# Last FFN of an encoder trunk: which PSUM sums its second projection keeps, and the order of its final norm

## The chip, the core and the metric

The kernel runs on one core of one Trainium2 chip. The metric is the device time of one execution in microseconds (us), the median of several runs. The profile comes from one further execution that the hardware profiler recorded. Its span runs from the first to the last instruction of the program on the core.

Names used below: TensorE (PE) multiplies matrices into PSUM, VectorE (DVE) and ScalarE (ACT) do elementwise work, GpSimd (POOL) and SyncE (SP) issue DMAs, and ACT can issue them too. Each engine works through its own queue in order.

## What is computed

The trunk has two layers. A layer is a half-step SwiGLU FFN, a gated pair of mixers, and another half-step FFN, each behind an RMSNorm and added to the residual x (512 tokens x 1024 columns, float32). Behind the last layer stands a final RMSNorm with a gain per column. The change is in the very last part of this:

```python
def rms_norm(x, g):
    xf = x.astype(jnp.float32)
    y = xf * lax.rsqrt(jnp.mean(xf * xf, axis=-1, keepdims=True) + RMS_EPS)
    return (y * g.astype(jnp.float32)).astype(x.dtype)

def swiglu(x, w_in, w_out):
    gu = x @ w_in
    g, u = jnp.split(gu, 2, axis=-1)
    return (jax.nn.silu(g) * u) @ w_out
...
        x = x + 0.5 * swiglu(rms_norm(x, ffn2_norm[l]), ffn2_w_in[l], ffn2_w_out[l])
    return rms_norm(x, final_norm)
```

## The kernel before

**Float32 by halves.** Every float32 operand is split into a high part and a low rest (`hi`, `lo`). A product of two of them is three matmuls: high by high (L508), low activations by high weights (L509), high activations by low weights (L511). For weights the split is made on the fly. Each granule of 128 x 1024 (some are 128 x 512) is loaded into a raw buffer (L148), ACT copies it to `whi` (L191), and DVE subtracts to get `wlo` (L194). Some granules are sums of two weight blocks: the second is added by an accumulating DMA from POOL (L150), or by DVE (L164). `whi` and `wlo` have three buffers each and raw nine, so a granule can be prepared at most about two granules ahead of PE. `Stream` walks a list of items in the order that `stage_items` (L199) wrote down. That list must match the order in which `product` (L513) asks for weights.

**The second projection of an FFN** multiplies 2816 features by 1024 columns with a Strassen-Winograd scheme: features, tokens and columns are each cut in two, and seven products take the place of eight. `x[j, i]` below is token half j (two blocks of 128 tokens) by column half i (512 columns). Each product runs over three chunks of features, c = 0, 1, 2, with two granules a chunk: 18 matmuls for c = 0 and 24 for c = 1 and 2. Each of them fills two PSUM banks, one for each block of 128 tokens.

The list `steps` (L758) sets the order: product 1 over its three chunks, product 2, then for each chunk 5, 6, 7, 3, and product 4 at the end. The operand of a step is combined by DVE (`comb`, L750), then split by ACT and DVE (L321, L322). `key` (L920) says which PSUM pair a product adds to: 6 goes on the sum of 1, and 4 on the sum of 7. Finished sums are added to x by `update` (L753, L756), one DVE instruction for each block:

| sum | goes to |
|---|---|
| 1 | x[0, 0], with a minus |
| 2 | x[0, 0] |
| 5 | x[1, 0], and x[1, 1] with a minus |
| 1 + 6 | x[1, 1]; x[1, 0] with a minus; x[0, 1] |
| 7 | x[1, 1] |
| 3 | x[1, 0] |
| 7 + 4 | x[0, 1] |

**The final norm.** `squares` (L371) has ACT sum the squares of one block and column half. Token half 1 (blocks 2 and 3) is complete before product 4 ends, token half 0 (blocks 0 and 1) only with it. The branch at L977 is written out by hand for DVE and ACT, and DVE comes to it behind the last `wlo`. For blocks 2 and 3, `inverses` (L445) makes the factor 1/rms in small steps. `gained` (L1022) multiplies half a row by the gain on DVE, `scaled` (L1029) multiplies a whole row of 1024 by 1/rms on ACT, and SP stores it (L1033). For blocks 0 and 1, `terms` (L424) prepares what is known of the first column half, and `inverse` (L431) finishes the factor: a square root on ACT, then four small DVE instructions (L438, L439, L441, L442). Block 0 ends with `gained` twice and `scaled`. Block 1 ends with `whole` (L1035) twice, a DVE instruction that applies gain and factor to half a row, and SP stores each half (L1040).

The last step, product 4 with c = 2, is done one token block after the other (`by_block`), so that block 0 is complete 12 matmuls before block 1.

**What orders the rest.** Outside of parts that are written out by hand, the order on ACT and DVE is the choice of a compile-time scheduler that goes by program order and readiness. At run time that order is fixed.

Of the kernel before, what the change touches and what calls it, by code (L numbers as in the profile page):

```python
# [14 lines left out]
AF = mybir.ActivationFunctionType  # L15
ALU = mybir.AluOpType
# [3 lines left out]
D = 1024  # L20
# [19 lines left out]
PLACE = {f: (h, c, i) for h in range(2) for c in range(3) for i, f in enumerate(CHUNK[h][c])}  # L40

# [49 lines left out]
def encoder_kernel(  # L91
# [107 lines left out]
    def stage_items():  # L199
# [39 lines left out]
        def ffn(s):  # L239
            first = not items  # L240
            if first:
                for g in range(4):
                    add(Raw((s, "cl", g)), parts=2 if g < 2 else 1, pieces=2 if g == 0 else 1)
            for j in range(NB):
                order = (1, 2, 5, 6, 7, 3, 4) if first and j == 0 else (1, 5, 6, 2, 7, 3, 4)
                strassen(s, lambda q: q, j, (1024,) * (2 if first or j else 3), order)
            for order in ((1,), (2,), (5, 6, 7, 3), (4,)):
                for c in range(3):
                    strassen(s, lambda q: "o" + q, c, out_sizes(c), order)
# [108 lines left out]
    class Norm:  # L358
# [65 lines left out]
        def terms(self, tb):  # L424

            e, f = small("e", 1), small("ef", 1)
            V.tensor_scalar(e, self.ssq[:, tb : tb + 1], 1.0 / D, EPS, ALU.mult, ALU.add)
            V.tensor_scalar(f, e, -0.5, None, ALU.mult)
            return e, f
# [185 lines left out]
    def stage_ffn(norm, nxt, late):  # L615
# [142 lines left out]
        steps = []  # L758
        for c in range(3):
            steps.append((1, c, lambda c=c: part(0, 0, c)))  # L760
        for c in range(3):
            steps.append((2, c, lambda c=c: part(1, 0, c)))
        for c in range(3):
            steps.append((5, c, lambda c=c: comb(part(0, 0, c), part(0, 0, c), part(0, 1, c), ALU.subtract)))
            steps.append((6, c, lambda c=c: comb(part(0, 0, c), part(0, 0, c), part(1, 1, c), ALU.add)))
            steps.append((7, c, lambda c=c: comb(part(0, 1, c), part(0, 1, c), part(1, 1, c), ALU.subtract)))
            steps.append((3, c, lambda c=c: part(1, 1, c)))
        for c in range(3):
            steps.append((4, c, lambda c=c: comb(part(1, 0, c), part(1, 0, c), part(0, 0, c), ALU.subtract)))
        made = {}  # L770

        def make(i):
            if i < len(steps) and i not in made:
                m, c, f = steps[i]
                made[i] = hl(f(), c, f"c{m}")
# [142 lines left out]
        for i, (m, c, _) in enumerate(steps):  # L918
# [3 lines left out]
            key = {6: 1, 4: 7}.get(m, m)  # L922
            if key not in ps:
                ps[key] = pair(f"o{key}")
            if m == 4 and c == 0 and nxt.mix:
# [4 lines left out]
                ps[key], made.pop(i), list(range(len(CHUNK[0][c]))), c == 0 and m in (1, 2, 3, 5, 7), c == 2,  # L930
                m in (4, 6), by_block=late and i == len(steps) - 1,
# [19 lines left out]
            if m == 4 and c == 1:  # L951
                update(ps[1], 1, 0, 1)
            if m == 4 and c == 0 and late:
                gf[0] = slot(F32, "gf", (D,))
                nc.sync.dma_start(out=gf[0], in_=bass.AP(tensor=gfin.tensor, offset=gfin.offset, ap=[[0, P], [1, D]]))
            if c < 2:
                continue
            if m == 1:
                update(ps[1], 0, 0, -1)
            elif m == 2:  # L960
                update(ps[2], 0, 0, 1)
                nxt.squares(0, 0)
            elif m == 5:
                update(ps[5], 0, 1, 1)
                update(ps[5], 1, 1, -1)
            elif m == 6:
                update(ps[1], 1, 1, 1)
            elif m == 7:
                update(ps[7], 1, 1, 1)
                nxt.squares(1, 1)  # L970
                update(ps[1], 0, 1, -1)
            elif m == 3:
                update(ps[3], 0, 1, 1)
                nxt.squares(0, 1)
                if late:
                    make(i + 3)
# [52 lines left out]
    def scaled(norm, tb):  # L1029
# [3 lines left out]
        nc.sync.dma_start(out=to, in_=o_)  # L1033

# [953 lines left out]
```

## Time and profile before

| what | value |
|---|---|
| time, median of 3 runs | 1858.4 us (1857.83 to 1858.85) |
| time of the profiled execution | 1859.64 us |
| its span, first to last instruction | 1857.9 us |
| PE busy | 1842.2 us (99% of the span) |
| DVE busy | 1605.6 us (86%) |
| ACT busy | 1311.2 us (71%) |
| POOL busy | 171.3 us (9%) |
| granted TensorE clock | 0.999 |

The profiled execution took 1.7 us more than its span, and 1.2 us more than the median of the runs. In the timeline view a row reads: start, duration, engine, line, operation, out<-in, shapes, count, and in brackets the idle time before it with what ended it. Where a row stands for several instructions (x2, x4), start is that of the first and the duration is from there to the end of the last. In tile names, `c5h` and `c5l` are the split operand of product 5, `o` on PE is the PSUM pair, `o` on DVE or ACT an output row, and `x` the residual.

### The profile page before, as it was taken

How to read it: one execution, taken by the hardware profiler on the slowest of the kernel's cores; microseconds unless marked ns; L12 is line 12 of the kernel's file. 1: busy time of each engine (PE TensorE's matmuls, PEld its weight loads, DVE VectorE, ACT ScalarE, POOL GpSimd, SP SyncE). 2: the span in 40 equal slices, each digit the busy share in tenths (PEclk: the TensorE clock that was granted, in tenths of full speed). 3: DMA queues.
4: the chain of work that ended last, by engine and by line, in shares of the span. 5: the costliest groups of instructions: out<-in, count | busy, mean ns of one | idle time of the engine just before them, and what ended most of it. 6: DMA issues, size and time to landing. Idle time of an engine off the chain costs nothing.

```text
span 1857.9 us, 24616 instructions
## 1 busy us (share of the span) xinstructions
PE 1842.2 (99%) x8862; PEld 1530.1 (82%) x8862; DVE 1605.6 (86%) x1950; ACT 1311.2 (71%) x1780; POOL 171.3 (9%) x210
## 2 busy tenths in 40 slices
PE   9999999999999999999999999999999999999997
PEld 7888878888888888888888888888888888888886
DVE  7878899786889987889998888998869899887898
ACT  6777875668676767777666778766675776777865
POOL 0001011100111010001010100101001101010010
PEclk9999999999999999999999999999999999999999
DMA  9898799932896788879888887988249867888794
GB/s 301 222 240 219 188 255 277 216 118 86 248 230 183 180 224 223 216 199 263 253 200 217 225 216 198 268 278 212 69 150 237 227 174 178 234 210 215 211 280 145
DMA packets 198458, 394.21 MB, mean 212 GB/s; under 512 B 103808, under 2 KB 103936, under 8 KB 198336
## 3 DMA queue, kind: packets, MB, share of 16 engines
q1 hardware_dynamic: 169664, 294.30, 49.2%
q0 software_dynamic: 28528, 98.33, 29.7%
q8 instruction: 69, 1.13, 0.3%
q14 instruction: 53, 0.43, 0.1%
q10 hardware_dynamic: 144, 0.02, 0.0%
HBM read 365.85 MB, written 2.11 MB: 198 GB/s over the span
## 4 chain that ended last, share of the span: by engine, by line
PE 88%; DVE 6%; DMA 2%; issue 2%; ACT 1%; SPq 0%; DVEq 0%; ACTq 0%
PE A L508 10%; PE A L511 10%; PE A L509 10%; PE B L509 5%; PE B L508 5%; PE B L511 5%; PE o L511 5%; PE o L509 5%; PE o L508 4%; PE ps L315 4%; PE ps L316 3%; PE ps L317 3%; PE C L508 3%; PE C L509 3%; PE C L511 3%
## 5 line engine op out<-in xcount | busy, mean ns | idle before, releaser
L194 DVE TENSOR_TENSOR wlo<-raw,whi 128x1024 fp32r<-128x1024 f32 (+1 forms) x534 | 632.0, 1195 | 172.8 <-ACT whi L191 171.3
L191 ACT ACTIVATE whi<-raw 128x1024 fp32r<-128x1024 f32 (+1 forms) x534 | 546.0, 1033 | 253.5 <-DVE raw L164 56.9
L150 POOL DMA_DIRECT2D raw<-in_wst_dram x166 | 144.2, 887 | 1339.3 <-DMA raw<-in_wst_dram 596.8
L164 DVE TENSOR_TENSOR raw<-raw,raw 128x1024 f32<-128x1024 f32 (+1 forms) x150 | 179.2, 1195 | 2.0
L509 PE MATMUL A<-whi,xl 128*128 128x512 f32 x400 | 155.7, 389 | 0.0
L508 PE MATMUL A<-whi,xh 128*128 128x512 f32 x400 | 155.7, 389 | 0.0
L356 ACT ACTIVATE at<-zt 128x1024 uint16<-128x1024 uint16 (+2 forms) x96 | 111.0, 1168 | 20.9 <-DMA zt<-zs 20.9
L186 ACT ACTIVATE whi<-raw 128x1024 fp32r<-128x1024 f32 (+1 forms) x83 | 85.9, 1035 | 46.9 <-issue 12.5
L511 PE MATMUL A<-wlo,xh 128*128 128x512 f32 x400 | 115.0, 389 | 0.0
L187 DVE SCALAR_TENSOR_TENSOR wlo<-raw,whi 128x1024 fp32r<-128x1024 f32 (+1 forms) x83 | 98.4, 1195 | 11.3 <-ACT whi L186 11.0
L511 PEld LDWEIGHTS A<-wlo,xh 128*128 128x128 f32 x400 | 75.1, 188 | 15.6
L508 PEld LDWEIGHTS A<-whi,xh 128*128 128x128 f32 x400 | 75.1, 188 | 15.4
L509 PEld LDWEIGHTS A<-whi,xl 128*128 128x128 f32 x400 | 75.1, 188 | 15.4
L508 PE MATMUL C<-whi,xh 128*128 128x512 f32 x208 | 81.1, 390 | 0.5 <-ACT whi L191 0.5
L509 PE MATMUL C<-whi,xl 128*128 128x512 f32 x208 | 81.0, 389 | 0.0
L509 PE MATMUL B<-whi,xl 128*128 128x512 f32 x208 | 81.0, 389 | 0.0
L508 PE MATMUL B<-whi,xh 128*128 128x512 f32 x208 | 80.9, 389 | 0.0
L730 ACT ACTIVATE th<-sn,rh 128x512 f32<-128x512 f32 x80 | 55.1, 715 | 36.2 <-DVE sn L583 35.4
L346 ACT ACTIVATE zs<-th 128x1024 uint16<-128x1024 uint16 x80 | 79.5, 1042 | 0.9 <-DVE th L737 0.9
L578 ACT ACTIVATE sn<-A 128x512 f32<-128x512 f32 x104 | 59.0, 584 | 24.9 <-PE A L511 24.9
L511 PE MATMUL B<-wlo,xh 128*128 128x512 f32 x208 | 59.8, 389 | 0.0
L511 PE MATMUL C<-wlo,xh 128*128 128x512 f32 x208 | 59.8, 389 | 0.0
(438 smaller groups left out, 4681.5 us busy)
## 6 DMA issues: line engine op xcount, KB each, us to landing
raw<-in_wst_dram SPq DMA_DIRECT2D x470, 512.0 KB, 5.7
raw<-in_wst_dram POOLq DMA_DIRECT2D x174, 512.0 KB, 8.0
raw<-in_wst_dram SPq DMA_DIRECT2D x30, 256.0 KB, 3.8
bm<-in_bias_dram SPq DMA_DIRECT2D x16, 384.0 KB, 3.5
x<-in_xin_dram SPq DMA_DIRECT2D x4, 512.0 KB, 10.2
raw<-in_wst_dram POOLq DMA_DIRECT2D x8, 256.0 KB, 8.4
dft<-in_dft_dram POOLq DMA_DIRECT2D x8, 256.0 KB, 4.3
gb<-in_gbias_dram SPq DMA_DIRECT2D x4, 512.0 KB, 14.8
```

The source lines that it names most:

```text
L150: G.dma_start(out=self.t, in_=wst[GRAN_AT[self.plus]][:, 0 : self.n], accum_op=ALU.add)
L164: V.tensor_tensor(self.raw.t, self.raw.t, self.add.t, ALU.add)
L186: S.activation(hi, t, AF.Copy, scale=-1.0)
L187: self.last = V.scalar_tensor_tensor(lo, t, -1.0, hi.bitcast(F32), ALU.mult, ALU.subtract)
L191: S.activation(hi[:, cs], t[:, cs], AF.Copy)
L194: self.last = V.tensor_tensor(lo[:, cs], t[:, cs], hi[:, cs].bitcast(F32), ALU.subtract)
L315: PE.matmul(ps, lh, rh, start=start, stop=False, skip_group_check=again)
L346: S.activation(s[:, h], words[:, h], AF.Copy)
L356: S.activation(to[:, w], t[:, w], AF.Copy)
L508: PE.matmul(ps, lh, rh, start=start, stop=False, skip_group_check=again)
L509: PE.matmul(ps, ll, rh, start=False, stop=False, skip_group_check=again)
L511: PE.matmul(ps, lh, rl, start=False, stop=stop, skip_group_check=again)
```

## The change

Four things change, all of them in the last FFN only (`late`), apart from code that is moved without effect.

1. Products 7 and 4 add to the PSUM pair of 1 and 6 (`key`). The sum 1 + 6 is read once, for x[1, 0]. After 7 it is read for x[1, 1], after 4 for x[0, 1]. So `update` is called twice less (four DVE instructions), and there is no pair for 7. Before product 7 may write the pair, the update after 6 must have read it, and before product 4 the update after 7.
2. The order of the products, of the weights and of their loads becomes: 1; 2 for c = 0, 1; 5, 6, 3 for each chunk; 7 for all chunks; 2 for c = 2; then 4. The chunk of product 2 stands between 7 and 4.
3. The factor for blocks 2 and 3 (`inverses`) and the prepared terms for blocks 0 and 1 (`terms`, now for both at once) are made during product 4, c = 0 and c = 1, ahead of the part that is written out by hand. The gain vector is loaded during product 7.
4. In the part written by hand, blocks 2 and 3 are finished first. For blocks 0 and 1, column half 0 is multiplied by the gain ahead of time and then scaled by ACT, which stores it from its own queue (`half_scaled`); column half 1 is finished by DVE (`whole`) and stored by SP.

```diff
+def out_order(last):
+
+    three = range(3)
+    if not last:
+        mid = [(m, c) for c in three for m in (5, 6, 7, 3)]
+        return [(1, c) for c in three] + [(2, c) for c in three] + mid + [(4, c) for c in three]
+    mid = [(m, c) for c in three for m in (5, 6, 3)] + [(7, c) for c in three]
+    return [(1, c) for c in three] + [(2, 0), (2, 1)] + mid + [(2, 2)] + [(4, c) for c in three]
...
-            for order in ((1,), (2,), (5, 6, 7, 3), (4,)):
-                for c in range(3):
-                    strassen(s, lambda q: "o" + q, c, out_sizes(c), order)
+            for m, c in out_order(s == (L - 1, 2)):
+                if m in (1, 2, 4, 5) or m == 7 and s == (L - 1, 2):
+                    group = {5: (5, 6, 3) if s == (L - 1, 2) else (5, 6, 7, 3)}.get(m, (m,))
+                    strassen(s, lambda q: "o" + q, c, out_sizes(c), group)
...
-            key = {6: 1, 4: 7}.get(m, m)
+            key = {6: 1, 7: 1 if late else 7, 4: 1 if late else 7}.get(m, m)
...
-            if m == 4 and c == 1:
+            if m == 4 and c == 1 and not late:
                 update(ps[1], 1, 0, 1)
-            if m == 4 and c == 0 and late:
+            if late and m == 7 and c == 1:
                 gf[0] = slot(F32, "gf", (D,))
...
+            if late and m == 4 and c < 2:
+                if c == 0:
+                    ready = nxt.inverses(2)
+                    next(ready)
+                    next(ready)
+                else:
+                    for _ in ready:
+                        pass
+                    ends = nxt.terms()
...
+                if late:
+                    make(i + 3)
...
+            elif m == 6 and late:
+                update(ps[1], 0, 1, -1)
             elif m == 6:
                 update(ps[1], 1, 1, 1)
             elif m == 7:
-                update(ps[7], 1, 1, 1)
+                update(ps[key], 1, 1, 1)
                 nxt.squares(1, 1)
-                update(ps[1], 0, 1, -1)
+                if not late:
+                    update(ps[1], 0, 1, -1)
...
-                    ready = nxt.inverses(2)
-                    next(ready)
-                    gained(2, 0)
-                    next(ready)
-                    gained(2, 1)
-                    for _ in ready:
-                        pass
-                    scaled(nxt, 2)
-                    update(ps[7], 1, 0, 1, (0,))
+                    for tb in (2, 3):
+                        gained(tb, 0)
+                        gained(tb, 1)
+                        scaled(nxt, tb)
+                    root = [nxt.inverse(b, *ends[b]) for b in range(2)]
+                    update(ps[1], 1, 0, 1, (0,))
                     nxt.squares(1, 0, (0,))
-                    root = [nxt.inverse(b, *nxt.terms(b)) for b in range(2)]
                     next(root[0])
-                    gained(3, 0)
-                    gained(3, 1)
-                    scaled(nxt, 3)
-                    update(ps[7], 1, 0, 1, (1,))
+                    gained(0, 0)
+                    gained(1, 0)
+                    update(ps[1], 1, 0, 1, (1,))
                     nxt.squares(1, 0, (1,))
                     next(root[1])
                     next(root[0])
-                    gained(0, 0)
                     next(root[0])
-                    gained(0, 1)
-                    scaled(nxt, 0)
+                    half_scaled(nxt, 0, 0)
+                    whole(nxt, 0, 1)
                     next(root[1])
                     next(root[1])
-                    whole(nxt, 1, 0)
+                    half_scaled(nxt, 1, 0)
                     whole(nxt, 1, 1)
...
+    def half_scaled(norm, tb, i):
+
+        o_, _, _, to = half(tb, i)
+        S.activation(o_, o_, AF.Copy, scale=norm.inv[tb])
+        S.dma_start(out=to, in_=o_)
```

In the file after the change, the added lines shift the numbers of those below them.

More of the change, by code (lines that the diff above doesn't have):

```diff
@@ L422, in gain, with terms @@
             return gn[:, c : c + 1]
-        def terms(self, tb):
-            e, f = small("e", 1), small("ef", 1)
-            V.tensor_scalar(e, self.ssq[:, tb : tb + 1], 1.0 / D, EPS, ALU.mult, ALU.add)
+        def terms(self):
+            e, f = small("e", 2), small("ef", 2)
+            V.tensor_scalar(e, self.ssq[:, 0:2], 1.0 / D, EPS, ALU.mult, ALU.add)
             V.tensor_scalar(f, e, -0.5, None, ALU.mult)
-            return e, f
+            return [(e[:, b : b + 1], f[:, b : b + 1]) for b in range(2)]
         def inverse(self, tb, e, f):
@@ L756, in update @@
                 V.scalar_tensor_tensor(v, ps[b], 0.25 * sign, v, ALU.mult, ALU.add)
[L758 to L769, printed above, removed]
+        operand = {
+            1: lambda c: part(0, 0, c),
+            2: lambda c: part(1, 0, c),
+            3: lambda c: part(1, 1, c),
+            5: lambda c: comb(part(0, 0, c), part(0, 0, c), part(0, 1, c), ALU.subtract),
+            6: lambda c: comb(part(0, 0, c), part(0, 0, c), part(1, 1, c), ALU.add),
+            7: lambda c: comb(part(0, 1, c), part(0, 1, c), part(1, 1, c), ALU.subtract),
+            4: lambda c: comb(part(1, 0, c), part(1, 0, c), part(0, 0, c), ALU.subtract),
+        }
+        steps = out_order(late)
         made = {}
@@ L773, in make @@
             if i < len(steps) and i not in made:
-                m, c, f = steps[i]
-                made[i] = hl(f(), c, f"c{m}")
+                m, c = steps[i]
+                made[i] = hl(operand[m](c), c, f"c{m}")
         def two(settle):
@@ L917, in stage_ffn @@
         ps = {}
-        for i, (m, c, _) in enumerate(steps):
+        for i, (m, c) in enumerate(steps):
             make(i)
@@ L929, in stage_ffn @@
             product(
-                ps[key], made.pop(i), list(range(len(CHUNK[0][c]))), c == 0 and m in (1, 2, 3, 5, 7), c == 2,
-                m in (4, 6), by_block=late and i == len(steps) - 1,
+                ps[key], made.pop(i), list(range(len(CHUNK[0][c]))), c == 0 and m in (key, 2), c == 2,
+                m != key, by_block=late and i == len(steps) - 1,
             )
@@ L974, in stage_ffn @@
                 nxt.squares(0, 1)
-                if late:
-                    make(i + 3)
             elif late:
```

## The prediction

> **What bounds the kernel now.** I read the page's totals first, then busy time by stretch around the end, then the timelines of the last FFN engine by engine.
>
> ```profile
> span 1857.9 us, 24616 instructions
> PE 1842.2 (99%) x8862; PEld 1530.1 (82%) x8862; DVE 1605.6 (86%) x1950; ACT 1311.2 (71%) x1780; POOL 171.3 (9%) x210
> ```
>
> ```profile
> 1754.00:1845.00 91.00, 91.00 (x403) 75.28 (x402) 89.25 (x95) 57.79 (x69) 10.03 (x12) 1.00 0.79 224
> 1848.40:1857.90 9.50, 0.00 (x0) 0.00 (x0) 4.97 (x14) 3.50 (x6) 0.00 (x0) 0.73 0.56 221
> ```
>
> PE is the bound: busy 99%, and in the second projection (first row, columns: length, then PE, PEld, DVE, ACT, POOL) 91.00 of 91.00 us. The change removes no matmul. So it can win only behind PE's end, in the 9.5 us of the second row, and it can lose wherever it makes PE wait. DVE with 89.25 of 91.00 us is next to full, so it is the engine that could do that. I work out the tail first, then the middle.
>
> **The tail.** PE's last matmul, two DVE and two ACT chains, and the stores:
>
> ```profile
> 1847.69 0.61 PE L511 MATMUL o<-wlo,c4h 128*128 128x512 f32 x2
> ```
>
> ```profile
> 1842.17 1.23 DVE L194 TENSOR_TENSOR wlo<-raw,whi 128x1024 fp32r<-128x1024 f32 x1
> ...
> 1847.62 1.28 DVE L1027 TENSOR_TENSOR o<-x,gf 128x512 f32<-128x512 f32 x2
> 1848.82 0.68 DVE L756 SCALAR_TENSOR_TENSOR x<-o,x 128x512 f32<-128x512 f32 x1
> ...
> 1850.63 0.68 DVE L1027 TENSOR_TENSOR o<-x,gf 128x512 f32<-128x512 f32 x1
> 1851.23 0.21 DVE L438 TENSOR_SCALAR mh<-ssq,ef 128x1 f32<-128x1 f32 x1
> ...
> 1852.10 1.42 DVE L1039 SCALAR_TENSOR_TENSOR o<-x,inv,gf 128x512 f32<-128x512 f32 x2
> ```
>
> ```profile
> 1848.94 1.15 ACT L1032 ACTIVATE o<-o,r 128x1024 f32<-128x1024 f32 x1 [0.21 <-DVE o L1027]
> 1849.99 0.61 ACT L375 ACTIVATE junk<-x 128x512 bf16<-128x512 f32 x1
> ...
> 1850.73 0.29 ACT L436 ACTIVATE sq<-ssq,e 128x1 f32<-128x1 f32 x1
> ```
>
> ```profile
> 1853.55 0.61 SPq L1040 DMA_DIRECT2D out_dram<-o  x1
> ```
>
> ```profile
> out_dram<-o SPq DMA_DIRECT2D x3, 512.0 KB, 2.6
> out_dram<-o SPq DMA_DIRECT2D x2, 256.0 KB, 2.9
> ```
>
> PE is through at 1847.69 + 0.61 = 1848.30; call this E. Before, three things then run late. DVE is still multiplying block 3 by the gain and starts the update of block 1 at 1848.82 (0.52 late). It ends at 1849.50, but ACT is scaling block 3 until about 1849.99 (0.45 late). Square root at 1850.73, out at 1851.02; DVE takes it at 1851.23, behind one more gain (0.21 late). The four small instructions take 1851.23 to 1852.10, 0.87. Then two halves, and the last store is issued at 1853.55.
>
> After, by the same durations. Behind the last `wlo` DVE has four gains (0.60 each, by 1.28 for two), 2.4 us, then the update of block 0, which is ready 12 matmuls or 2.7 us ahead of E, and two gains, 1.2 us. The last `wlo` ends at 1843.40 before. Were it no earlier, this would end at 1843.40 + 2.4 + 0.6 + 1.2 = 1847.6, ahead of E. The update of block 1 thus starts at E: 1848.30 to 1848.98. ACT's two scalings of 1.15 and the squares of block 0 are over before that too. So squares at 1849.02, 0.74 on (1849.99 to 1850.73) the root at 1849.76, out at 1850.05. DVE in the meantime: block 0's four small ones from 1848.90 to 1849.77, block 0's half (1.42 for two: 0.67 to the next start, 0.75 for the last) to 1850.44, block 1's four, 0.87, to 1851.31, and its half, 0.75, to 1852.06. Store issued near 1852.1: **1.45 us earlier** (0.52 and 0.45 of lateness gone, block 1's factor 0.18 later behind the root than before, one half of 0.67 out of the chain).
>
> ACT's halves beside this: 512 columns cost between the 0.61 of squares and the 1.15 of 1024 columns; I take 0.61, same size. Block 0's runs 1850.08 to 1850.7, then ACT issues its store. A store issued by ACT isn't in this tail; the nearest is a load that ACT issues at the start:
>
> ```profile
> 0.74 0.39 ACTq L1826 DMA_DIRECT2D gn<-in_gains_dram  x1
> ```
>
> That is 0.39, SP's last store 0.61; either way ACT is free by 1851.3, when block 1's factor is out, and its half ends at 1851.95 with the issue at 1852.0. Beside DVE's half, so free. Landing: before, the last three stores, one row of block 0 and two halves of block 1, crowd together; after, only the last two halves do, with block 0's 1.5 us ahead of them. By the two rows a store lands 2.6 us after issue by itself and 2.9 in the crowd, so 0 to 0.3 is won; I take 0.3. The tail gives **1.75 us**, or 1.45 without this.
>
> On that last 0.3 the Trainium skill speaks against it. Its page "DMA: Bandwidth & Descriptors", section "Issuing engines are not separate DMA queues", says that DMAs from SP and ACT run on the same 16 DMA engines and interleave, so a second issuing engine saves only the time to issue. By that the two last halves land together as half a MB would, the 0.3 shrinks towards 0, and the forecast below would read 1857.5. The rows lean that way (halves 2.9, whole rows 2.6), but can't show it, since no two queues store at once before.
>
> **The middle: does PE still never wait?** What the order costs is DVE's work against PE's.
>
> ```profile
> 1789.61 0.39 PE L508 MATMUL o<-whi,c5h 128*128 128x512 f32 x1
> ...
> 1805.96 0.39 PE L508 MATMUL o<-whi,c3h 128*128 128x512 f32 x1
> ```
>
> ```profile
> 1817.63 1.22 DVE L194 TENSOR_TENSOR wlo<-raw,whi 128x1024 fp32r<-128x1024 f32 x1
> 1818.77 2.48 DVE L756 SCALAR_TENSOR_TENSOR x<-o,x 128x512 f32<-128x512 f32 x4
> 1821.16 1.22 DVE L194 TENSOR_TENSOR wlo<-raw,whi 128x1024 fp32r<-128x1024 f32 x1
> ```
>
> Products 5, 6 and 7 of one chunk lie between the two PE rows: 72 matmuls in 16.35 us, 0.227 each, 5.45 a product. On DVE an instruction of 1024 columns takes the place of 1.14 us (1817.63 to 1818.77), an update 0.60 (four from 1818.77 to 1821.16).
>
> A chunk in the order 5, 6, 3 needs 6 `wlo`, 4 sums of weights, 3 rests of operands and 2 combinations: 15 x 1.14 = 17.1 us against 16.35 of PE, 0.75 short. With product 7 in it, as before, it is 19 x 1.14 = 21.7 against 21.8, even. For c = 0, with 0.87 and 0.60 for its smaller sizes, 13.05 against 54 x 0.227 = 12.25, 0.8 short. Then four updates after 5 and two after 6: 3.6. In all 0.8 + 2 x 0.75 + 3.6 = 5.9 us short when product 7 starts, and PE now must wait there for those two updates. Product 7 gives it back (4 x 1.14 = 4.55 against 5.45). Some of this is done ahead:
>
> ```profile
> 1744.89 0.95 DVE L750 TENSOR_TENSOR at<-at,at 128x768 f32<-128x768 f32 x1
> 1745.76 1.22 DVE L750 TENSOR_TENSOR at<-at,at 128x1024 f32<-128x1024 f32 x1
> ...
> 1757.58 1.22 DVE L750 TENSOR_TENSOR at<-at,at 128x1024 f32<-128x1024 f32 x1
> ```
>
> These three must be product 5's, by what they may read so early: 0.87 + 2 x 1.14 = 3.15. So 2.75 us short. And the lead that DVE has to lose, from a `wlo`'s end to its first matmul:
>
> ```profile
> 1769.59 1.22 DVE L194 TENSOR_TENSOR wlo<-raw,whi 128x1024 fp32r<-128x1024 f32 x1
> ...
> 1797.17 1.24 DVE L194 TENSOR_TENSOR wlo<-raw,whi 128x1024 fp32r<-128x1024 f32 x1
> ```
>
> ```profile
> 1775.10 1.07 PE L511 MATMUL o<-wlo,c5h 128*128 128x512 f32 x4
> ...
> 1798.68 0.63 PE L511 MATMUL o<-wlo,c6h 128*128 128x512 f32 x2
> ```
>
> At product 5's first granule it is 1775.10 - 1770.81 = 4.3 us, at 6's last of c = 1 it is 1798.68 - 1798.41 = 0.27. So the lead shrinks by 4.0 before, where the count above says even: DVE also takes up combinations that aren't due. After, 5 comes a product earlier (5.45) and only 3.4 (two `wlo`, one rest) + 1.2 of DVE's work moves behind it: 0.85 less. The bounds are then 4.3 - 0.85 - 2.75 = 0.7 us left, no stall, and 4.0 less than that, a stall of 3.3. I take **0.6 us of stall**, one update's slot, since the nearest row (0.27) shows a lead near nothing with no stall. The four updates that go save 2.4 us of DVE; on the path that is worth nothing, since PE doesn't wait for them, beyond the lead it restores behind product 7. A wait of product 7 costs its full length, since every later matmul stands behind it on PE. Product 4's wait for the update after 7 has a chunk of product 2, 5.45 us, in between: two updates (1.2) fit, so nothing.
>
> What moves behind product 7: its updates 1.2, those of product 2 1.2, and `inverses` and `terms`, eight small DVE instructions of at most 0.21 (the L438 row), 1.7; 4.1 in all. Spare there on DVE: 5.45 - 3.4 in product 2's chunk, 0.6, 0.9 and 0.9 in product 4's, 4.45. So they are hidden; without that cover the last `wlo` comes later, of which the first 0.7 (1847.6 against E) is free. ACT, 57.79 us of 91, has room for the squares that move. Of loads none is added; the gain vector's half MB moves into product 7, on SP's queue, and is counted in (b).
>
> **Sum.** 1857.9 - 1.75 + 0.6 = 1856.75 for the span, -1.15. The profiled execution took 1859.64, 1.2 above the median of 1858.4; I take the difference to the median: **1857.2**.
>
> **Rivals.**
> (a) *DVE runs out of lead and product 7 waits for its update.* The place is the end of 6 and 3, c = 2, and the start of 7, c = 0; it decides once the lead at 6, c = 2 is under the 3.6 of updates. For it: 0.27 before. Against: DVE's total is smaller. Price 3.3, so -1.75 + 3.3 = +1.55, 1859.9, slower; where the updates' 3.6 come on top, +5.15, 1863.5.
> (b) *Transfers.* Rows of the DMA view from 1780 to 1820 (packets, MB, share of the time of 16 engines):
>
> ```profile
> q0 software_dynamic: 1107, 4.01, 51.6%
> q1 hardware_dynamic: 2277, 8.06, 51.3%
> ```
>
> A granule of 0.52 MB takes 0.516 x 40 x 0.52 / 4.01 = 2.7 us when accumulated and 1.3 when loaded plainly. Product 7 needs two of each, 8.0 us against 5.45; three of them in a row fall 2.0 (c = 0) + 2 x 2.6 = 7.2 behind, and 1.3 more with the gain vector. The chunks of 5, 6, 3 (13.4 against 16.35) gain 2.9 each ahead of it, as far as nine buffers allow. If only one chunk's 2.9 is kept, beside half of the 4.3 of lead, 7.2 + 1.3 - 2.9 - 2.15 = 3.45 us of stall: +1.7, 1860.1; with neither, 8.5: +6.75, 1865.1.
> (c) *The tail is hardly shortened.* If an ACT half costs the whole row's 1.15 and each issue 0.61 of ACT's time, block 0's half and store hold ACT from 1850.08 to 1851.84, block 1's half ends at 1853.0, and the last store is issued 0.55 earlier than before, not 1.45. With the stall that is +0.05, 1858.4: the change then does nothing.
> (d) No stall, and all of the tail: 1856.6.
>
> **Chances.** Forecast (with d) 0.60, (a) 0.24, (b) 0.08, (c) 0.08. The likeliest case's own range is 1856.1 to 1858.6 ((d) less half a microsecond, the runs' own spread, to a stall of 2). For 8 in 10 I reach to (b), (c) and the cheaper (a): 1855.8 to 1861.2. Bounds of 0.2% (3.7 us), about what a measurement of this kernel can tell from no change, are 1854.7 and 1862.1: faster 0.05 (only what I overlook), slower 0.15 (the dear end of (a), and the rest of (b)), same 0.80.
>
> **What would show it.** The update of block 1 starts within 0.1 of PE's end, the squares directly behind it, the last store is issued 3.8 us behind PE's end (5.25 before). PE idle in the second projection is under 1.5 us; if there is more, the row behind the gap names DVE (a) or a DMA under ACT's `whi` (b). A last store later than 4.5 behind E shows (c). The forecast is wrong if the gaps are many, or if the tail keeps one of its three delays.

## The result, and the profile after

| kernel | median of its runs, us | ratio to before | 95% interval |
|---|---|---|---|
| before, beside it | 1858.12 (6 runs) | | |
| changed | 1864.68 (6 runs, 1862.43 to 1868.31) | 1.0034 | 1.0024 to 1.0045 |

The changed kernel is slower by 0.3%, outside the forecast range. Its profiled execution took 1862.43 us, the fastest of its six, so the profile shows the smaller part of the loss: a span of 1860.7 beside 1857.9, 2.8 us more. From the page's totals of the changed kernel:

```profile
PE 1843.1 (99%) x8862; PEld 1529.1 (82%) x8862; DVE 1603.4 (86%) x1944; ACT 1311.7 (70%) x1781; POOL 171.3 (9%) x210
```

The totals say nothing: PE is at 99% in both. The stretch of the second projection does (length, then PE, PEld, DVE, ACT, POOL). Before, PE was busy in 91.00 of these 91 us:

```profile
1754.00:1845.00 91.00, 86.98 (x374) 69.17 (x374) 85.05 (x95) 57.07 (x69) 8.63 (x10) 1.00 0.78 228
```

PE lacks 4.02 us, and DVE is busy for 85.05 us where it was 89.25 before: it is no longer full either. The view of PE's waits in that stretch (who waits, for whom, us in total, times, longest) has no row at all for the kernel before, and these for the changed one:

```profile
PE o L519 <- ACT c7h L332: 1.1, 1, 1.1
PE o L519 <- ACT whi L201: 1.1, 1, 1.1
PE o L522 <- DVE wlo L204: 1.1, 1, 1.1
PE o L520 <- DVE c7l L333: 0.7, 1, 0.7
```

There are four waits, at three places: near 1761, near 1790, and at product 7's last chunk near 1825. The timeline of the changed kernel around them, and around its end:

```profile
1744.44 9.83 SPq L358 DMA_TRANSPOSE zt<-zs  x2
1745.12 0.86 POOL L160 DMA_DIRECT2D raw<-in_wst_dram  x1 [41.58 <-DVE at L761]
1747.55 0.86 POOL L160 DMA_DIRECT2D raw<-in_wst_dram  x1 [1.57 <-DVE wlo L197]
...
1756.64 1.37 ACT L367 ACTIVATE at<-zt 128x1024 uint16<-128x1024 uint16 x1 [3.64 <-DMA zt<-zs]
...
1758.51 0.69 DVE L204 TENSOR_TENSOR wlo<-raw,whi 128x512 fp32r<-128x512 f32 x1 [3.55 <-ACT whi L201]
...
1761.63 0.50 PE L519 MATMUL o<-whi,c2h 128*128 128x512 f32 x1 [1.07 <-ACT whi L201]
...
1790.51 0.73 PE L522 MATMUL o<-wlo,c6h 128*128 128x512 f32 x2 [1.05 <-DVE wlo L204]
...
1823.64 1.06 ACT L201 ACTIVATE whi<-raw 128x1024 fp32r<-128x1024 f32 x1 [2.30 <-DMA raw<-in_wst_dram]
...
1824.61 1.04 ACT L332 ACTIVATE c7h<-at 128x1024 fp32r<-128x1024 f32 x1
...
1825.70 0.73 PE L519 MATMUL o<-whi,c7h 128*128 128x512 f32 x2 [1.14 <-ACT c7h L332]
1827.15 0.50 PE L520 MATMUL o<-whi,c7l 128*128 128x512 f32 x1 [0.72 <-DVE c7l L333]
...
1852.22 0.61 PE L522 MATMUL o<-wlo,c4h 128*128 128x512 f32 x2
1852.87 0.69 DVE L767 SCALAR_TENSOR_TENSOR x<-o,x 128x512 f32<-128x512 f32 x1 [0.82 <-PE o L522]
...
1855.88 0.72 ACT L1053 ACTIVATE o<-o,inv 128x512 f32<-128x512 f32 x1 [0.63 <-DVE inv L453]
...
1856.63 0.37 ACTq L1054 DMA_DIRECT2D out_dram<-o  x1
```

**The end** went as forecast. PE is through at 1852.22 + 0.61 = 1852.83. The update of block 1 starts 0.04 behind it, the last store is issued 3.80 behind it (5.25 before), and the span ends 7.87 behind it (9.60 before): 1.73 us won. But PE itself ends 4.53 us later than before's 1848.30, and 4.53 - 1.73 is the 2.8 of the span.

**Near 1761** the reader is to follow the chain upward. PE waits for a `whi` of ACT. ACT had stood 3.64 us, with that `whi` queued behind it, at the copy `at<-zt`, which waits for a pair of transposing DMAs, the first of them issued by SP at 1744.44. DVE stood 3.55 us for the same ACT. Beside SP's transposes POOL issues two accumulating loads, at 1745.12 and 1747.55. In the changed order of weights these are product 5's first two granules. Before, the same loads came behind the transposes:

```profile
1745.42 3.33 SPq L347 DMA_TRANSPOSE zt<-zs  x1
1749.48 3.47 SPq L347 DMA_TRANSPOSE zt<-zs  x1
1753.68 0.86 POOL L150 DMA_DIRECT2D raw<-in_wst_dram  x1 [47.67 <-DVE c1l L322]
1755.08 1.38 ACT L356 ACTIVATE at<-zt 128x1024 uint16<-128x1024 uint16 x1 [0.58 <-DMA zt<-zs]
1756.53 0.86 POOL L150 DMA_DIRECT2D raw<-in_wst_dram  x1 [1.99 <-DVE wlo L194]
```

The view of the tile `zt` gives the transposes' time from issue to landing, for the changed kernel and then for the one before:

```profile
DMA to landing us min/median/max: 8.6/8.8/9.0
```

```profile
DMA to landing us min/median/max: 5.3/5.4/5.6
```

Beside the accumulating loads the transposes take 3.4 us longer.

**At 1825** ACT waits 2.30 for a raw granule of product 7, `c7h` stands behind that `whi` in ACT's queue, and PE waits for `c7h` and then for DVE's `c7l`. The DMA view of the changed kernel from 1805 to 1826 (packets, MB, share of 16 engines' time):

```profile
q1 hardware_dynamic: 1278, 4.39, 53.3%
q0 software_dynamic: 580, 2.10, 50.5%
```

The two kinds add up to all that 16 engines have. The four accumulating loads, 2.10 MB, take 0.505 x 21 = 10.6 us, 2.65 a granule.

Counted from one matmul's start to the next, less the usual 0.227, the gaps of the changed kernel are 1.5 us near 1761, 1.2 near 1790, 2.2 near 1825 and 0.35 elsewhere, 5.2 in all, where the kernel before has one of 0.70 at 1752. Behind each gap one more interval is 0.1 longer. From its first matmul to its last the projection takes 111.08 us (1741.36 to 1852.44), before 105.57 (1742.35 to 1847.91): 5.5 us more. PE ends only 4.53 later because this execution came to the projection 0.99 earlier, from parts that are the same in both kernels.

The wait near 1790 can't be read from one profile: DVE is late with a `wlo`, and it may have been late by its own count or by the 3.55 us that it lost at 1758. That is for the experiments.

### The profile page after: what moved, and what is told of

It reads as the page before. It is cut to its first block, busy times and chain, and to the rows that moved or that the text cites. A ratio compares the mean times of both kernels' runs of the same rounds, so it can differ in the third digit from the quotient of the medians.

```text
span 1860.7 us, 24610 instructions
## 1 busy us (share of the span) xinstructions
PE 1843.1 (99%) x8862; PEld 1529.1 (82%) x8862; DVE 1603.4 (86%) x1944; ACT 1311.7 (70%) x1781; POOL 171.3 (9%) x210
## 4 chain that ended last, share of the span: by engine, by line
PE 88%; DVE 4%; DMA 3%; issue 3%; ACT 1%; POOL 0%; SPq 0%; DVEq 0%; ACTq 0%; POOLq 0%
PE A L519 10%; PE A L522 10%; PE A L520 10%; PE o L522 5%; PE o L520 5%; PE o L519 5%; PE B L520 5%; PE B L519 5%; PE B L522 5%; PE ps L326 4%; PE ps L327 3%; PE ps L328 3%; PE C L520 2%; PE C L519 2%; PE C L522 2%
```

## The experiments

The theory after this reading: two bursts of accumulating loads cost the time, one by holding up the transposes, one by being late themselves, and the wait at 1790 is an echo of the first. The rival: DVE's work ahead of product 7 is too much, as rival (a) of the prediction has it, and the loads are only beside it. Each time is compared with runs of the kernel before on the same chip: 1860.03 (23 runs) for the two halves, for the kernel without product 7's second block and for product 2 at its old place; 1859.46 (27) for the changed kernel once more, for the kernels without product 5's second block and without both, and for 7 and 2 in turn; 1859.21 (29) for product 5 summed by DVE, one chunk of 2 ahead, and the end with one issuing engine.

### The two halves of the change, each alone

The first kernel has the old order of products, weights and sums, and the new last rows; the second has the new order and the old last rows. The core of the first, against the changed kernel (the second is its counterpart):

```diff
-    mid = [(m, c) for c in three for m in (5, 6, 3)] + [(7, c) for c in three]
-    return [(1, c) for c in three] + [(2, 0), (2, 1)] + mid + [(2, 2)] + [(4, c) for c in three]
+    mid = [(m, c) for c in three for m in (5, 6, 7, 3)]
+    return [(1, c) for c in three] + [(2, c) for c in three] + mid + [(4, c) for c in three]
...
-            key = {6: 1, 7: 1 if late else 7, 4: 1 if late else 7}.get(m, m)
+            key = {6: 1, 4: 7}.get(m, m)
```

> The kernel before with only the norm's part of the change: factor and terms made early, blocks 2 and 3 first, the last rows in halves by ACT and DVE. Products, sums and weights keep their old order. Theory (the loss of the changed kernel is all in the middle, the tail gains 1.7): PE ends where it does before, from PE's end to the end of the span 7.8 us in place of 9.6, and the time is 1.5 to 1.8 us below the kernel before. Rival (the tail needs the four updates gone): DVE is late at the last weights, PE waits up to 1 us, and the gain is under 0.8 us.

> The changed kernel with the old order of the norm's tail: products 7 and 4 on the sum of 1 and 6 and the new order of weights alone. Theory: PE ends 4 to 7 us later than before, as in the changed kernel, and the time is 5 to 8 us above the kernel before. Rival (the early norm steps and the moved gain vector in the middle make the gaps): PE ends within 1.5 us of before, time within 1.5 us.

The new end alone: 1859.14 (11 runs), ratio 0.9996, 0.9987 to 1.0004. Its span is 1856.1, PE waits for nothing from 1754 on, as before, and from the last matmul's start to the span's end are 8.39 us, 9.95 before: 1.56 won. The median is 0.9 us below before, not the 1.5 to 1.8 expected; the interval holds both that gain (0.08%) and no change.

The new order alone: 1872.25 (5 runs), ratio 1.0061, 1.0048 to 1.0074. That is 11 to 12 us above before, more than the 5 to 8 expected, and PE's last matmul starts 7.5 later than before (1855.45). So the loss is in the order, and neither the early norm steps nor the new end are needed for it. Its waits in the profile are those of the changed kernel, at the same places (near 1762, 1790 and 1825 to 1828). But one thing is added behind the last one. The busy times of the stretch behind it (length, PE, PEld, DVE, ACT, POOL, then the granted clock, the DMA share and GB/s):

```profile
1829.50:1833.00 3.50, 3.50 (x10) 2.67 (x10) 2.73 (x4) 1.21 (x2) 0.00 (x0) 0.51 0.29 112
```

PE waits for nothing here, yet its granted clock is 0.51, and its matmuls start 0.427 us apart where they otherwise start 0.227 apart. That adds about 3.5 x (1 - 0.227 / 0.427) = 1.6 us.

### The changed kernel once more

> The changed kernel unaltered, for a second profile and on the same chip as the next three. Theory (part of the loss is PE's granted clock: where its waits in product 7 add up to about 2.4 us, the clock is halved for some 3.5 us behind them, 1.4 us more): the waits stand at the same places, near 1760, 1789 and 1825, and a profile that is longer than the first has a stretch of clock near 0.5 behind the last of them; time 4 to 8 us above the kernel before. Rival (the longer runs come from transfers alone): the clock stays at 1.00 throughout, and the longer profile has longer waits.

1866.41 (5 runs), ratio 1.0042, 1.0029 to 1.0055. This profiled execution, 1865.98 us, has the same waits near 1761 and 1790, and at product 7 a longer one, again with the low clock behind it. The two waits at 7 from the view of PE's waits, and the stretch behind them:

```profile
PE o L519 <- ACT c7h L332: 3.0, 1, 3.0
...
PE o L520 <- DVE c7l L333: 0.7, 1, 0.7
```

```profile
1829.50:1833.00 3.50, 3.50 (x11) 2.69 (x10) 2.64 (x3) 1.74 (x2) 0.00 (x0) 0.53 0.19 73
```

Here the two waits at 7 are 1.9 longer than in the first profile (3.0 beside 1.1), and the clock adds about 1.6. Together that is 3.5 of the 3.9 us by which the projection is longer (115.03 beside 111.08); the spans differ by 3.5 (1864.2 and 1860.7). Executions of this kind would lift the median above the first profile, but how many of the runs are like it no profile shows.

### Each burst without its accumulating loads

Three kernels leave the second weight block out: of product 7's granules, of product 5's first two, and of both. The order and all other work stay.

```diff
 # product 7
-            for q, q2 in (("a", None), ("b", None), ("c", "a"), ("d", "c")):
+            for q, q2 in (("a", None), ("b", None), ("c", None if order == (7,) else "a"), ("d", "c")):
...
 # product 5, c = 0
-            for q, q2 in (("a", None), ("b", None), ("c", "a"), ("d", "c")):
+            for q, q2 in (("a", None), ("b", None), ("c", "a"), ("d", None if order == (5, 6, 3) and idx == 0 else "c")):
```

> The changed kernel, but product 7's weights are loaded without adding their second block, so that part of its sum is left out. Three products 7 in a row then need 2.7 us of transfers each, not 8. Theory (transfers): the gap of 2.3 us at product 7, c = 2, goes, and the spread of the times with it; time 2 to 5 us below the changed kernel. Rival (DVE's lead): ACT and DVE are late at product 7 in any case, the gap stays over 1.5 us, and the time falls by less than 1 us.

> The changed kernel, but the two granules of product 5, c = 0, are loaded without adding their second block, so that part of its sum is left out. Theory (these two accumulating loads hold up the transposes, ACT waits 3.6 us behind them, and DVE idles with it): ACT's wait for the transposed words near 1753 falls under 1 us, the PE gap near 1760 goes, and the gap of 1.2 us near 1790 goes too, since it comes from the lead that DVE lost there; PE ends 2 to 2.7 us earlier than in the changed kernel. Rival (DVE's own count of work in 5, 6, 3 makes the gap near 1790): that gap stays, and PE ends only 0.8 to 1.5 us earlier.

> Both loads left plain: product 5's, c = 0, and all of product 7's, whose second blocks are left out of the sums. Theory (two bursts of accumulating loads make all of the loss): PE waits under 0.7 us in the whole projection, and the time is 1 to 2 us below the kernel before, the tail's gain. Rival (DVE is short by itself): 1.2 us or more of waits for DVE's results remain, time within 1 us of the kernel before.

Without product 7's: 1863.85 (12 runs), ratio 1.0022, 1.0011 to 1.0033. PE's waits from 1754 on:

```profile
PE o L519 <- ACT whi L201: 1.4, 2, 1.2
PE o L522 <- DVE wlo L204: 1.1, 1, 1.1
```

Both rows of product 7 are gone, those near 1761 and 1790 stay, and against before beside it the time is about 0.1 to 0.2% lower than the changed kernel's, the low end of the 2 to 5 us expected. Without product 5's first two: 1859.64 (11 runs), ratio 1.0008, 0.9999 to 1.0017, with these waits, and this landing of the transposes:

```profile
PE o L519 <- ACT c7h L332: 1.5, 1, 1.5
PE o L520 <- DVE c7l L333: 0.7, 1, 0.7
```

```profile
DMA to landing us min/median/max: 4.3/4.7/5.0
```

Now it is the other way round, and the row of 1790 went with that of 1761 although nothing was taken from DVE's work. So the wait at 1790 was an echo, and the rival (DVE's own count) falls for this order. PE's last matmul starts 2.8 us earlier than in the changed kernel, a little more than the 2 to 2.7 expected. Without both: 1857.12 (11 runs), ratio 0.9987, 0.9978 to 0.9996, and in the second projection one wait of 0.2 us is left:

```profile
PE o L520 <- DVE c7l L333: 0.2, 1, 0.2
```

From its first matmul to its last the projection takes 5.5 us more than before in the changed kernel, 4.4 without product 7's blocks, 2.3 without product 5's, and 0.1 less than before without both (105.46). So the two bursts make the whole loss of the projection; the savings of each alone sum to 4.3 and not 5.6, since with one burst gone the gaps at the other are longer (2.6 beside 2.2 at product 7, 2.2 beside 1.5 near 1761). The median is 2.3 us below before beside it, where the forecast had 1.2; that its number is within 0.1 us of the forecast's 1857.2 says nothing, since this kernel leaves work out and ran on another chip. (The profiled execution of this kernel was a long one, 1862.13 us, with 2.0 us of waits near 1301, in an earlier part that no kernel here touches; the row above is of the second projection alone.)

### The chunk of product 2 back at its old place

Products 5, 6 and 3 come one chunk later again, and 4 follows directly on 7.

```diff
-    return [(1, c) for c in three] + [(2, 0), (2, 1)] + mid + [(2, 2)] + [(4, c) for c in three]
+    return [(1, c) for c in three] + [(2, c) for c in three] + mid + [(4, c) for c in three]
...
                 update(ps[2], 0, 0, 1)
                 nxt.squares(0, 0)
-                if late:
-                    make(i + 3)
...
                 update(ps[key], 1, 1, 1)
                 nxt.squares(1, 1)
+                if late:
+                    make(i + 3)
```

The second part moves with it: the operand three steps on is now combined behind 7 and not behind 2.

> The changed kernel with product 2's last chunk back in its old place, ahead of 5, so that nothing stands between 7 and 4. Theory (the first accumulating loads of 5 run beside the two transposing DMAs and hold them up): the gap of 1.5 us near 1760 goes, since these loads are issued behind the transposes again; in its place PE waits 1 to 1.5 us at the start of 4 for the update of 7; time within 1.5 us of the changed kernel. Rival (the gap near 1760 has nothing to do with the order of loads): the gap stays, and the wait at 4 comes on top, 1 to 2 us above the changed kernel.

1867.94 (5 runs), ratio 1.0043, 1.0032 to 1.0055. The waits near 1761 and 1790 are gone (ACT waits 0.49 for `zt`), but the new one at product 4 is far larger than expected:

```profile
1840.06 1.28 DVE L767 SCALAR_TENSOR_TENSOR x<-o,x 128x512 f32<-128x512 f32 x2
1840.89 0.77 PE L519 MATMUL o<-whi,c4h 128*128 128x512 f32 x1 [4.60 <-DVE x L767]
```

```profile
1840.90:1846.60 5.70, 5.70 (x14) 4.44 (x15) 3.02 (x6) 2.43 (x6) 0.00 (x0) 0.50 0.00 0
1846.60:1852.00 5.40, 5.40 (x25) 4.46 (x24) 4.05 (x9) 2.22 (x3) 0.00 (x0) 1.00 0.00 0
```

The update for which 4 waits is queued on DVE behind weight rests and combinations that product 7's late loads had held back: ACT waits 2.64 us for a raw granule until 1831.82, DVE 2.47 for ACT until 1832.91, and then DVE has seven instructions to go through before the update at 1840.06. The granted clock is 0.50 for the 5.7 us that follow, 14 matmul records where the next 5.4 us have 25. My sum of 1 to 1.5 us had only the update in it, not the queue ahead of it. That the time is within 1.5 us of the changed kernel's by the two ratios, as expected, is luck: one wait went and a dearer one came.

### Product 5's first granules summed by DVE

DVE makes the two sums in place of the accumulating loads, and the second block is loaded plainly.

```diff
+            by_dve = order == (5, 6, 3) and idx == 0
-            for q, q2 in (("a", None), ("b", None), ("c", "a"), ("d", "c")):
+            for q, q2 in (("a", None), ("b", None), ("c", "a"), ("d", None if by_dve else "c")):
...
-                    add(d)
+                    add(d, Raw(key("c", g), sizes[g]) if by_dve else None)
```

> The changed kernel, in which the second block of product 5's first two granules is loaded plainly into raw buffers and added by DVE, so that the same result is computed without the accumulating loads that ran beside the transposing DMAs. Theory (those loads hold the transposes up): ACT waits under 1 us for zt, the gaps near 1760 and 1790 go as they did with the block left out, the gap at product 7 stays at 1.5 to 2.5 us, and TensorE's last matmul starts 2 to 2.7 us ahead of the changed kernel's 1852.44: time 0 to 2 us above before. Rival (DVE has no room there): two more sums of 0.8 to 0.9 us each put TensorE to wait for DVE by 1 us or more between 1755 and 1800, and the time is as the changed kernel's, 5 us or more above before.

1861.98 (11 runs), ratio 1.0018, 1.0009 to 1.0026: 2.8 above before, so neither in the theory's 2 nor at the rival's 5. The waits other than those at product 7, and the landing:

```profile
...
PE o L521 <- DVE c1l L334: 0.9, 1, 0.9
...
PE o L523 <- DVE wlo L204: 0.3, 1, 0.3
```

```profile
DMA to landing us min/median/max: 5.2/5.6/6.0
```

The same bytes loaded plainly at about the same place leave the transposes at 5.6 us. So the mere bytes don't hold them up. The accumulating loads differ in two things, their kind and their way in (POOL's queue, where the plain loads go through SP's), and no run here separates these. ACT still waits 1.54 for `zt`, more than the 1 us that I expected at most: the second transpose is issued at 1750.20, behind two of the plain loads in SP's queue, 0.7 later than before. A `c1l` is 0.9 late at 1753 (0.70 of a gap was there before too) and a `wlo` 0.3 at 1790. PE's last matmul starts at 1852.09, only 0.36 ahead of the changed kernel's first profile, not 2 to 2.7. Of the rest 1.1 us is no effect of the edit: this execution came to the projection that much later (1742.49 beside 1741.36), and the projection itself is 1.5 us shorter (109.60 beside 111.08).

### Other places for product 2 and 7

The first order has 7 and 2 in turn behind all of 5, 6 and 3, the second has one chunk of 2 ahead of 5.

```diff
+    mid = [(m, c) for c in three for m in (5, 6, 3)] + [(m, c) for c in three for m in (7, 2)]
+    return [(1, c) for c in three] + mid + [(4, c) for c in three]
...
+    mid = [(m, c) for c in three for m in (5, 6, 3)] + [(7, 0), (2, 1), (7, 1), (7, 2)]
+    return [(1, c) for c in three] + [(2, 0)] + mid + [(2, 2)] + [(4, c) for c in three]
```

> The changed kernel with product 2's three chunks between those of product 7: 1; 5, 6, 3 for each chunk; 7, 2 in turn; 4. The whole reference is computed. Theory (transfers at 7 and at the transposes): 7 and 2 together need 10.6 us of transfers in 10.9, so no wait for loads there; the accumulating loads of 5, c = 0, are issued ahead of the transposes. The gaps near 1760 and 1825 go, at most 1.5 us of waits for DVE remain, time 0 to 2 us below the kernel before. Rival (DVE's lead): with 5, 6, 3 begun two products sooner DVE has no lead at all, PE waits 3 us or more in 5 to 3, time 2 us or more above the kernel before.

> The whole reference is computed. Product 1, one third of product 2, then 5, 6 and 3 in turn, then 7, 2, 7, 7, 2 in thirds, then 4: product 5's accumulating loads come a block later than in the changed kernel and product 7's are partly spread. Theory (both bursts of accumulating loads are the cause, not DVE's count of work): no gap near 1760 beyond the 0.7 that before has, ACT waits under 1 us for zt, DVE's gaps between 1760 and 1815 sum to under 1.5 us beside 2.6 with 7 and 2 in turn behind all of 5, 6 and 3, the wait at the last third of 7 is under 1 us, and with the new tail's 1.5 us the time is 0 to 2 us below before. Rival (two 7s in a row are enough to make their loads late): 1 us or more of waiting for raw at the last third of 7, time 0 to 2 us above before.

In turn: 1859.92 (11 runs), ratio 1.0005, 0.9996 to 1.0014; with one chunk of 2 ahead: 1860.51 (11 runs), 1.0007, 0.9999 to 1.0016. In neither does PE wait at product 7, and in the second the accumulating loads come at 1759.48, behind the transposes, which land in 5.6 us. Both bursts are dealt with. But neither kernel is faster than before, where the two expectations had them 0 to 2 us below it. What is left in the first is 2.5 us of small gaps before 1815 (1.5 expected at most), all for results of DVE, in the second 0.9 at product 4's start and mostly this (PE's longest wait, then the timeline around it):

```profile
PE o L520 <- DVE c6l L333: 2.3, 2, 1.6
```

```profile
1780.07 1.22 DVE L204 TENSOR_TENSOR wlo<-raw,whi 128x1024 fp32r<-128x1024 f32 x1
...
1781.21 1.22 DVE L333 TENSOR_TENSOR c6l<-at,c6h 128x1024 fp32r<-128x1024 f32 x1
...
1782.48 0.50 PE L520 MATMUL o<-whi,c6l 128*128 128x512 f32 x1 [1.58 <-DVE c6l L333]
```

This is DVE. It goes from one instruction to the next without a pause, and PE waits for its `c6l`. My expectation of under 1.5 us was wrong: the gaps before 1815 are 0.93, 0.14, 1.75 and 0.71, 3.5 in all. DVE's lead runs out when product 5 comes two chunks earlier than before, and not when it comes one earlier. The mechanism of rival (a) is real, one chunk farther on than I had put it.

### The end with one issuing engine

The old order with the new end, with ACT's halves stored through SP:

```diff
-        S.dma_start(out=to, in_=o_)
+        nc.sync.dma_start(out=to, in_=o_)
```

> The kernel with the old products and the new last rows, with one thing changed: the output halves that ACT finishes are stored through SP instead of by ACT itself. It tests what the second issuing engine is worth, which the prediction took as 0.3 us of landing and which a page read the other way makes 0 of landing. Theory: SP, which issues the other half's stores too, gets to the last one 0.35 to 0.6 us later (one issue of 0.35 to 0.37 us stands ahead of it), so that from the last matmul's start to the span's end are 8.7 to 9.0 us beside 8.39 with ACT's own stores, and the time stays within 0.6 us of what tail_only gave, 1 us below before. Rival: the two engines' stores run at the same time only from two issuers, and 1 us or more of the gain is lost: 9.4 us or more, the time as before.

1858.11 (12 runs), ratio 0.9994, 0.9985 to 1.0003. The last stores of the kernel with ACT's own issues, then of this one:

```profile
1850.55 1.87 SPq L1055 DMA_DIRECT2D out_dram<-o  x2
1850.56 0.36 ACTq L1048 DMA_DIRECT2D out_dram<-o  x1
...
1852.06 0.37 ACTq L1048 DMA_DIRECT2D out_dram<-o  x1
```

```profile
1850.97 0.33 SPq L1055 DMA_DIRECT2D out_dram<-o  x1
...
1851.40 1.42 SPq L1048 DMA_DIRECT2D out_dram<-o  x2
...
1852.91 0.41 SPq L1055 DMA_DIRECT2D out_dram<-o  x1
```

Counted from the last matmul's start (1847.70 and 1847.79), the last store is issued 0.76 us later with SP alone (5.12 beside 4.36), but the span ends only 0.32 later (8.71 beside 8.39). The end is at the low edge of the 8.7 to 9.0 expected. Two engines that issue at once win 0.76 of issuing, and 0.44 of that goes again in landing. That agrees with what the Trainium skill says in "DMA: Bandwidth & Descriptors", section "Issuing engines are not separate DMA queues": the second issuer saves issuing time and nothing else.

## Why the prediction was wrong

**The end: right.** Each step came as summed. The update of block 1 starts 0.04 behind PE's end (0 foreseen), the last store 3.80 behind it (3.8), and 1.73 us is won (1.75). ACT's half takes 0.72, not 0.61, but starts with DVE's half, which takes 0.75, so nothing hangs on it. The Trainium skill's rule ("DMA: Bandwidth & Descriptors", "Issuing engines are not separate DMA queues") has it right that a store does not land sooner for it: from the end of the last issue to the span's end are 3.70 us, 3.74 before. The 0.3 that I put down to landing is there, but it is the shorter last issue, 0.37 us in place of 0.61.

**The middle: this is the step that failed.** For "I take **0.6 us of stall**" the projection took 5.5 us more than before in the first profile and 9.5 in the second, of which about 1.6 is the low clock (PE ended 4.5 and 8.1 later than before). The bounds of 0 to 3.3 were bounds of DVE's count alone, and DVE's count was not what decided. With both bursts of accumulating loads away the same order had one wait of 0.2 us: for DVE alone the 0.6 was near enough, and its lead sufficed.

**What was left out.** "Of loads none is added" is true, and I stopped there. Moving a load moves what it meets. In the trace of before I had the rows to see it: the transposes at 1745.42 and 1749.48 and product 5's accumulating loads at 1753.68, which had to come earlier by a chunk, 5.45 us, at least. I did not look at that place, since the change is not there. It cost 1.5 us near 1761 and 1.2 at 1790.

**Rival (b)** had the right mechanism for the other burst: three 7s in a row want 8.0 us of transfers in 5.45 of PE, and the measured 2.65 us a granule is the 2.7 of its sum. Its price, 3.45, lies between the 2.2 and 4.1 that the two profiles show at product 7. It got 0.08 since I let the nine raw buffers and DVE's lead stand against it; of the 8.5 us that it counts without them they covered more than half, but not all. The gain vector that it counts has no part in the first profile's wait: its load is issued at 1823.27, 0.37 before ACT gets its granule (and was issued at 1825.36 in the kernel before). **Rival (a)** did not occur: PE never waits for the update at product 7's start in the changed kernel. Of **(c)** nothing is seen.

**Product 4's wait: nothing, as foreseen**, and the experiment with 4 directly behind 7 shows what that order avoids: a wait of 4.6 us.

**Not foreseen at all** is the low clock behind a wait, about 1.6 us in the second profile.

**What stays open.** The new order alone loses 0.6%, more than the changed kernel's 0.3 to 0.4% and the end's 1.6 us explain together; its profiled execution, 1866.73, is the fastest of its five and has a stretch of low clock already, so what puts the median 5.5 us higher is not seen. The runs of the kernel without product 7's second block lie between 1861 and 1870 us, and its profile, of an execution of 1862.07, does not show why. And of the kernels that leave no work out none beats the one before clearly: the old order with the new end, in two versions, is 0.04 and 0.06% below it, and both intervals reach past 1.

## What to carry to other kernels

When an order of work changes, list where each moved transfer is issued before and after, and what else is being moved at that time, even far from the edit; a count of loads (none added here) misses it. Price bursts of the dear kind of load (here 2.65 us a granule when accumulated, 1.3 when plain) against the time of the work that they feed, and count how much of a burst the buffers cover before letting them stand against it. And when a wait lies on the engine that bounds, price what it does behind it too.

## What the runs showed of the hardware

**Accumulating loads from POOL hold up SP's transposing DMAs.** Median time of the two transposes of `zt` from issue to landing, and ACT's wait for them:

| accumulating loads of product 5, c = 0 | kernel | landing, us | ACT's wait, us |
|---|---|---|---|
| behind the transposes | before | 5.4 | 0.58 |
| beside them | changed, two profiles | 8.8, 9.5 | 3.64, 4.09 |
| beside them | new order alone | 8.8 | 3.30 |
| beside them | product 7 plain | 9.6 | 4.51 |
| plain loads and sums by DVE | product 5 by DVE | 5.6 | 1.54 |
| left out | product 5 plain | 4.7 | none |
| behind the transposes | one chunk of 2 ahead | 5.6 | 0.69 |
| behind the transposes | product 2 back | 5.4 | 0.49 |
| ahead of the transposes | 7 and 2 in turn | 4.5 | none |

**The granted clock can halve behind short waits of PE.** Behind 4.1 us of waits in two parts (the second profile of the changed kernel) and behind the 4.6 at product 4 it did; behind 2.4 us in two parts (the new order alone, 1.54 and 0.88) it did as well, and so did it near 1303 behind 2.0 in two parts in the kernel with both bursts plain; behind 2.2 (the changed kernel's first profile) and 2.6 (product 5 plain), each in two parts too, it did not. In the second projection it stays at 0.50 to 0.53 for 3.5 to 5.7 us. The Trainium skill, "TensorE: Matmul & The Clock Gate", Part 1, has a clock gate that halves the clock after an idle window of about 3.4 us; the window runs freely. The matmuls' 0.427 us at 512 columns is its figure for the low clock (426.7 ns). Of the waits here only the one at product 4 is longer than that window and agrees with it; in the others no part is over 3.2 us, so waits that are shorter and broken by two matmuls can suffice, and between 2.0 and 2.6 us the runs here have both outcomes.
